# A hybrid SSD, DeltaNet and attention backbone: two-head attention units and chain loads two tiles ahead

## The chip, the cores and the metric

One core of a Trainium2 chip runs the whole program. The metric is the device time of one execution in microseconds; lower is better.

## What is computed

The reference is a backbone of two layers. Each layer normalises and modulates 256 context tokens and 2048 latent tokens, projects them from 1024 to 3100 columns, runs three groups of heads side by side, joins them, projects back and adds the result to the stream. The groups are a state-space scan in both directions (SSD, 6 heads), a gated DeltaNet scan in both directions (4 heads), and softmax attention (6 query heads on 2 key heads, over context and latents). Everything is float32. The attention part, which most of the change is about:

```python
s = jnp.einsum('bqhgd,bkhd->bhgqk', qi, k).astype(jnp.float32) * scale
pr = jax.nn.softmax(s, axis=-1).astype(v.dtype)
return jnp.einsum('bhgqk,bkhd->bqhgd', pr, v)
```

and the DeltaNet recurrence over chunks of 64 tokens, which is serial:

```python
v_new = u_i - jnp.einsum('bhcd,bhde->bhce', w_i, S)
o = jnp.einsum('bhcd,bhde->bhce', qd, S) + jnp.einsum('bhij,bhje->bhie', a_i, v_new)
S = S * d_i[..., None, None] + jnp.einsum('bhcd,bhce->bhde', kd, v_new)
```

## The kernel before, in words

Tokens are cut into 18 tiles of 128 (2 of context, 16 of latents). A layer first runs the input projection (L401, L455), then gating, `gdn_pre` and `gdn_solve` (DeltaNet's triangular systems, on VectorE at L987 and L989 and on GpSimd at L993 and L995), `ssd_states` and `ssd_out` (SSD), `gdn_chain` (the recurrence, tile by tile, both directions at once), and last the output projection (L1231) with the next layer's modulation. Attention is written as generators and runs between all of these.

The order of the instructions on each engine isn't written out. The tile framework schedules them before the program runs, by a timeline of its own, and the order is then fixed; each engine takes its instructions in that order and waits on semaphores. The first eight attention units of a layer stand ahead of `gdn_chain` in the program (L1189) and the rest behind it (L1193).

A unit of attention is one head and 512 queries: 24 such units per layer, and in layer 0 also 6 small ones of 256 context queries. `unit_max` (L516) loads the queries (`q2`, their high parts over their low parts), copies the high half to `qm` on GpSimd (L522), multiplies them with the keys in 20 pieces (`pq`, L531) and takes each piece's maximum over keys on VectorE (`mx`, L533). Small reductions and a sign change give the negated maximum of each query (`nm`, L535, L536); four small fp32 products with the identity turn it into a row (`pm`, L541), which VectorE copies into row 64 of `qm` (L542). `unit_main` (L545) then makes the scores of each of 18 key tiles in two fp32r products (`pst`, L562 and L563; the second brings in the low parts and the negated maximum), takes the exponential on ScalarE (`pe`, L565) and sums the values with these weights (`po`, L556). `v1` holds 65 columns per key head: 64 of the value and one of ones, so that the row sums come out of the same product.

The sum over values comes in two forms. Units 0 to 12 multiply `pe` in plain fp32, one product per tile, which the trace shows as two instructions. From unit 13 on, `pe` and `v1` are split into a high and a low fp32r part (`ph` on ScalarE, L570, `pl` on VectorE, L571; `vh` at L653), and three fp32r products take the place of the fp32 one:

```python
ops = [(v1, pe)] if ph is None else [(vh[0], ph), (vh[1], ph), (vh[0], pl)]
```

In `gdn_chain`, `prep(u)` loads a tile's data through the SP queue (`acv` and others, L1048 to L1055) into pools of two buffers, scales it on VectorE and GpSimd (L1056 to L1061), and makes two sets of 32x32 products on TensorE (`pv`, L1067 and L1076). `step(u)` runs the two halves of a tile; a half takes three turns from TensorE to another engine and back (L1100 to `r` on VectorE; L1114 to `V` on ScalarE; L1123 to `Sc` on VectorE). The loop calls `prep(u + 1)` ahead of `step(u)`:

```python
cur, nxt = nxt, prep(u + 1) if u + 1 < NT else None
S, ox = step(u, S, *cur)
```

`ssd_states` has a product with 64 columns of weights: L789 writes two 64-column halves of one PSUM tile, one after the other, each with 128 rows of weights and 192 moving columns. In `ssd_out`, L816, L839, L840, L845 and L857 are VectorE's part of each tile, and L813, L832, L849, L850, L822 and L858 GpSimd's.

## Time and profile before

| | us |
|---|---|
| median of 3 runs (lowest, highest) | 4039.15 (4035.92, 4040.36) |
| the profiled execution's own time | 4035.59 |
| its span, first to last instruction | 4033.8 |
| TensorE busy (share) | 3776.4 (94%) |
| VectorE busy (share) | 2720.7 (67%) |
| ScalarE busy (share) | 1800.4 (45%) |
| GpSimd busy (share) | 1351.1 (33%) |
| mean granted TensorE clock, share of 2.4 GHz | 0.969 |

PE is TensorE, PEld its loading of weights, DVE VectorE, ACT ScalarE, POOL GpSimd, SP the queue that issues most transfers. Matmuls are pipelined: a row's duration runs from issue to the end and overlaps with the next one's, so what one of them occupies is read from the starts of the rows that follow. The granted clock is a share of 2.4 GHz; its other level is 1.2 GHz, so a mean between 0.5 and 1 is a mix of stretches at either.

### The profile page before, as it was taken

What the parts mean: (1) busy time and instruction counts of PE and PEld (TensorE: products, weight loads), DVE (VectorE), ACT (ScalarE), POOL (GpSimd) and SP (SyncE); (2) the same over time, 40 slices, a digit from 0 to 9 for tenths busy, and PEclk for the clock granted to TensorE, in tenths of its full rate; (3) what the DMA queues carried; (4) which work ended last, traced back from release to release, by engine and by line L of the source; (5) the groups of instructions that cost most, each with busy time, mean ns of one, the idle gap of its engine ahead of it and who ended that gap; (6) DMA issues with size and microseconds to landing.
All of it is one profiled execution on the core that took longest, in us unless ns stands there. A gap on an engine that the chain in (4) does not pass through costs nothing. (4 is left out here: it accounts for less than half of the span.)

```text
span 4033.8 us, 70483 instructions
## 1 busy us (share of the span) xinstructions
PE 3776.4 (94%) x25750; PEld 2839.4 (70%) x25750; DVE 2720.7 (67%) x5372; ACT 1800.4 (45%) x3728; POOL 1351.1 (33%) x1760
## 2 busy tenths in 40 slices
PE   7999999999999888897999999999898999888989
PEld 5899999554566556565678999996554665556667
DVE  6556573789977567774547574746888776667733
ACT  5343332443466455564214443423333655556610
POOL 5112130477476221321213030303774662123100
PEclk9999999999999889998999999999999999989999
DMA  6343432345222544535744433332452215444344
GB/s 202 98 144 112 133 105 95 104 151 173 69 60 60 111 105 103 116 73 181 241 153 130 152 111 130 118 100 77 144 175 72 61 55 118 101 104 120 85 140 154
DMA packets 549798, 477.72 MB, mean 118 GB/s; under 512 B 133128, under 2 KB 487372, under 8 KB 549452
## 3 DMA queue, kind: packets, MB, share of 16 engines
q1 hardware_dynamic: 507596, 437.82, 37.1%
q10 hardware_dynamic: 41856, 35.40, 2.9%
q8 instruction: 203, 3.33, 0.3%
q14 instruction: 143, 1.17, 0.1%
HBM read 328.91 MB, written 144.18 MB: 117 GB/s over the span
## 5 line engine op out<-in xcount | busy, mean ns | idle before, releaser
L565 ACT ACTIVATE pe<-pst 128x512 f32<-128x512 f32 (+1 forms) x876 | 511.8, 594 | 692.0 <-PE pst L563 654.3
L533 DVE TENSOR_REDUCE mx<-pq 128x1 f32<-128x512 f32 (+1 forms) x972 | 590.6, 626 | 131.1 <-PE pq L531 127.0
L531 PE MATMUL pq<-khh,q 128*128 128x512 f32 (+1 forms) x972 | 459.9, 498 | 38.7 <-DVE mx L533 32.1
L556 PE MATMUL po<-pe,v 128*65 128x512 f32 x960 | 488.5, 597 | 0.8 <-ACT os__11676 L579 0.8
L562 PE MATMUL pst<-q,khh 128*128 128x512 f32 (+1 forms) x876 | 429.3, 490 | 16.8 <-DVE mx L533 14.0
L455 PE MATMUL ps<-lo,wh 128*128 128x384 f32 (+2 forms) x1296 | 441.3, 340 | 0.0
L455 PE MATMUL ps<-hi,wl 128*128 128x384 f32 (+2 forms) x1296 | 441.0, 340 | 0.0
L455 PE MATMUL ps<-hi,wh 128*128 128x384 f32 (+2 forms) x1296 | 440.9, 340 | 0.0
L571 DVE TENSOR_TENSOR pl<-pe,ph 128x512 fp32r<-128x512 f32 x396 | 309.6, 786 | 118.6 <-ACT ph L570 54.3
L563 PE MATMUL pst<-qm,klo 65*128 65x512 f32 (+1 forms) x876 | 356.9, 408 | 0.0
L401 PE MATMUL ps<-wh,hi 128*128 128x320 f32 (+1 forms) x1120 | 354.4, 318 | 0.1
L401 PE MATMUL ps<-wl,hi 128*128 128x320 f32 (+1 forms) x1120 | 350.8, 314 | 0.0
L401 PE MATMUL ps<-wh,lo 128*128 128x320 f32 (+1 forms) x1120 | 350.2, 315 | 0.5 <-DVE lo L366 0.5
L531 PEld LDWEIGHTS pq<-khh,q 128*128 128x128 f32 x972 | 186.7, 195 | 190.2 <-DVE mx L533 73.6
L570 ACT CAST ph<-pe 128x512 fp32r<-128x512 f32 x396 | 243.8, 620 | 94.0 <-PE po L556 36.4
L376 DVE TENSOR_TENSOR wl<-wt,wh 128x1024 fp32r<-128x1024 f32 (+3 forms) x144 | 175.3, 1246 | 160.2 <-ACT wh L375 159.8
L556 PE MATMUL po<-ph,vh 128*65 128x512 f32 x792 | 262.2, 413 | 7.7 <-ACT os__20088 L579 4.6
L562 PEld LDWEIGHTS pst<-q,khh 128*128 128x128 f32 x876 | 171.3, 196 | 128.7 <-issue 53.5
L455 PEld LDWEIGHTS ps<-lo,wh 128*128 128x128 f32 x1296 | 244.0, 188 | 10.8 <-issue 0.4
L455 PEld LDWEIGHTS ps<-hi,wh 128*128 128x128 f32 x1296 | 243.5, 188 | 10.3
L455 PEld LDWEIGHTS ps<-hi,wl 128*128 128x128 f32 x1296 | 243.4, 188 | 10.3
L1231 PE MATMUL psd<-woh,mh 128*128 128x512 f32 x544 | 218.7, 402 | 19.0 <-ACT mh L1222 17.6
(588 smaller groups left out, 8136.4 us busy)
## 6 DMA issues: line engine op xcount, KB each, us to landing
wt<-in_w_in_dram SPq DMA_DIRECT2D x72, 512.0 KB
wmt<-in_w_mod_dram SPq DMA_DIRECT2D x48, 512.0 KB
pre_d<-pre SPq DMA_DIRECT2D x34, 512.0 KB
acv<-pre_d SPq DMA_DIRECT2D x34, 512.0 KB
kqc<-kt_d SPq DMA_DIRECT2D x68, 256.0 KB
acv<-pre_d SPq DMA_DIRECT2D x68, 256.0 KB
wt<-in_w_in_dram SPq DMA_DIRECT2D x24, 668.0 KB
wt<-in_w_in_dram SPq DMA_DIRECT2D x24, 640.0 KB
```

The source lines that it names most:

```text
L376: nc.vector.tensor_tensor(out=wl[:, ks, :], in0=wt, in1=wh[:, ks, :].bitcast(F32), op=ALU.subtract)
L401: nc.tensor.matmul(ps, hh[:, k, a], ww[:, k, :], start=(n == 0), stop=(n == 3 * KD - 1))
L455: nc.tensor.matmul(ps, ww[:, k, m * P:(m + 1) * P], hh[:, k, s0:s0 + sn], start=(n == 0), stop=(n == 3 * KD - 1))
L531: nc.tensor.matmul(pq[:, :n], q2[:, u * P:(u + 1) * P], khh[:, kvh, k0t * P + a:k0t * P + a + n], start=True, stop=True)
L533: nc.vector.tensor_reduce(mx[:, i:i + 1], pq[:, :n], axis=AX.X, op=ALU.max)
L556: nc.tensor.matmul(po[0:65, :qn], v[:, kt, vs], p[:, :qn], start=(kt == k0t and j == 0), stop=(kt == k1t - 1 and j == len(ops) - 1))
L562: nc.tensor.matmul(pt[:, :qn], khh[:, kvh, ks], q2[:, :qn], start=True, stop=False)
L563: nc.tensor.matmul(pt[:, :qn], klo[:, kvh, ks], qm[:, :qn], start=False, stop=True)
L565: nc.scalar.activation(out=pe[:, :qn], in_=pt[:, :qn], func=AF.Exp, scale=0.125)
L570: nc.scalar.copy(out=ph, in_=pe)
L571: nc.vector.tensor_tensor(out=pl, in0=pe, in1=ph.bitcast(F32), op=ALU.subtract)
L1231: nc.tensor.matmul(ps, a, w[k][:, n * 512:n * 512 + 512], start=(k == 0 and i == 0), stop=(k == KD - 1 and i == 2))
```

## The change

Units 0 to 7 stay single, now always in plain fp32. The other 16 become eight pairs of two neighbouring heads (`pair_max`, `pair_main`). A pair makes the scores of both heads for a key tile, with two exponentials into one tile `pe` of 128x2x512. Its value products are plain fp32 with 64 columns each, one head into partitions 0 to 63 of `po` and the other into 64 to 127. They are issued in visits of two key tiles, four products in a row, tied behind the last score product. The row sums no longer come out of these products: VectorE adds each new `pe` to `acc` (17 additions of 128x1024 per pair), and at the end two products with ones sum `acc` over its partitions. The splits into `ph`, `pl` and `vh` are gone.

In `unit_max`, `qm`'s high half comes by a second transfer instead of a copy on GpSimd; one reduction per unit takes the place of four and the sign change, and writes into column 64 of a tile that is otherwise zero; the four products that turn it are fp32r with 65 columns of weights; ScalarE copies the row instead of VectorE.

In `gdn_chain`, the transfers of a tile move out of `prep` into `load`, which is called two tiles ahead, and their pools get three buffers.

```diff
-                qm = ap_.tile([65, 512], F32R, name="qm", bufs=3)
-                nc.gpsimd.tensor_copy(qm[0:64, :qn], q2[0:64, :qn].bitcast(F32))
+                    nc.sync.dma_start(qm[0:64, :qn].bitcast(F32), qt_d[0:64, h, q0:q0 + qn])
...
-                    nc.vector.tensor_reduce(nm[:, u:u + 1], mx[:, 0:len(pieces)], axis=AX.X, op=ALU.max)
-                nc.vector.tensor_scalar(out=nm[:, :qn // P], in0=nm[:, :qn // P], scalar1=-1.0, scalar2=None, op0=ALU.mult)
+                nz = nmz[next(turn) % 2]
+                nc.vector.tensor_reduce(nz[:, 0:nu, 64:65], mx[:, 0:nu, 0:len(pieces)], axis=AX.X, op=ALU.max, negate=True)
...
-                    nc.tensor.matmul(pm[64:65, u * P:(u + 1) * P], nm[:, u:u + 1], ident, start=True, stop=True)
-                nc.vector.tensor_copy(qm[64:65, :qn], pm[64:65, :qn])
+                    nc.tensor.matmul(pm[0:65, u * P:(u + 1) * P], nz[:, u, :], identr, start=True, stop=True)
+                nc.scalar.copy(out=qm[64:65, :qn], in_=pm[64:65, :qn])
...
+            def pair_main(h0, q0, qn, k0t, k1t, st):
...
+                def visit(n, behind_mm):
+                    with tc.high_priority():
+                        for v in range(n):
+                            kt, pe = pend.pop(0)
+                            for j in range(2):
+                                c0 = kvh[j] * 65
+                                mm = nc.tensor.matmul(po[half[j]], v1[:, kt, c0:c0 + 64], pe[:, j], start=(kt == k0t), stop=(kt == k1t - 1))
+                                if v == 0 and j == 0:
+                                    behind(mm, behind_mm)
...
+                    pe = ap_.tile([P, 2, 512], F32, name="pe", bufs=PB)
+                    for j in range(2):
+                        pt = aslot("pst")
+                        nc.tensor.matmul(pt, khh[:, kvh[j], ks], st["q2"][j], start=True, stop=False)
+                        mm = nc.tensor.matmul(pt, klo[:, kvh[j], ks], st["qm"][j], start=False, stop=True)
+                        nc.scalar.activation(out=pe[:, j], in_=pt, func=AF.Exp, scale=0.125)
...
+                        nc.vector.tensor_tensor(out=acc, in0=acc, in1=pe, op=ALU.add)
+                    pend.append((kt, pe))
+                    if len(pend) == 3:
+                        visit(2, mm)
...
+                for j in range(2):
+                    nc.tensor.matmul(pl[half[j]], cc("ones")[:, 0:64], acc[:, j], start=True, stop=True)
...
+                units = [(1, un) for un in big[:NS]] + [(2, un) for un in big[NS::2]]
...
+                        xt = gw.tile([P, 2, 4, 32], F32, name="xt_", bufs=3)
+                        kq = gw.tile([P, 2, 4, P], F32, name="kqc", bufs=3)
+                        er = gw.tile([P, 4, P], F32, name="er", bufs=3)
+                        acv = gw.tile([P, 2, 4, 4, 64], F32, name="acv", bufs=3)
...
-                    nxt = prep(0)
+                    ahead = [load(0), load(1)]
+                    nxt = prep(*ahead.pop(0))
                     for u in range(NT):
-                        cur, nxt = nxt, prep(u + 1) if u + 1 < NT else None
+                        if u + 2 < NT:
+                            ahead.append(load(u + 2))
+                        cur, nxt = nxt, prep(*ahead.pop(0)) if ahead else None
```

How the scheduled order moves, at three places. The first is TensorE in the chain of layer 0. Before, the split products of a unit (`po<-ph`, `po<-pl`) stand between the chain's products (`p<-Sc`) and those of a tile's preparation (`pv<-xt`):

```order
L562 MATMUL pst<-q_17963,khh 128x512
L563 MATMUL pst<-qm,klo 128x512
L556 MATMUL po<-ph,vh_17036 65x512
L556 MATMUL po<-ph,vh_17037 65x512
L1067 MATMUL pv<-xt__14053,acv 32x32
L1100 MATMUL p<-Sc,kqc 64x64 x8
L1109 MATMUL p<-Sc,kqc 64x64 x2
L556 MATMUL po<-pl,vh_17036 65x512
L556 MATMUL po<-ph,vh_17036 65x512
L556 MATMUL po<-ph,vh_17037 65x512
L556 MATMUL po<-pl,vh_17036 65x512
```

and now:

```order
L1127 MATMUL pv<-xt__14553,acv 32x32 x16
L613 MATMUL pst<-q_17550,khh 128x512
L614 MATMUL pst<-qm,klo 128x512
L613 MATMUL pst<-q_17704,khh 128x512
L614 MATMUL pst<-qm,klo 128x512
L604 MATMUL po<-pe,v_352 64x512 x4
L613 MATMUL pst<-q_17550,khh 128x512
```

Three products per key tile and head have become one (L604, four in a row for two tiles and two heads). The preparation's first product, of which before one stood alone with other work behind it and the other 15 followed later, now stands with all its 16 together.

The second place is VectorE during SSD in layer 0, one tile's stretch. L840, L839, L845, L857 and L816 belong to SSD, L533 and L535 to attention. Before:

```order
L533 TENSOR_REDUCE mx<-pq 128x1 x2
L857 TENSOR_TENSOR t_9703<-py,t_9703 128x384
L816 SCALAR_TENSOR_TENSOR m_9881<-cst,sp,m_9881 128x128 x6
L533 TENSOR_REDUCE mx<-pq 128x1
L839 TENSOR_TENSOR m_9788<-m_9788,pd 128x384
L845 TENSOR_TENSOR t_9796<-po_9820,ecum 128x192
L845 TENSOR_TENSOR t_9797<-po_9820,ecum 128x192
L861 TENSOR_SCALAR sq<-sq 128x1
L840 TENSOR_TENSOR m_9788<-m_9788,ee 128x384
L533 TENSOR_REDUCE mx<-pq 128x1 x2
```

and now (L896, L895, L901, L913 and L872 are the same lines of SSD; L538 is the maximum and L624 the addition):

```order
L624 TENSOR_TENSOR acc<-acc,pe 128x1024
L538 TENSOR_REDUCE mx<-pq 128x1 x2
L913 TENSOR_TENSOR t_9611<-py,t_9611 128x384
L538 TENSOR_REDUCE mx<-pq 128x1
L872 SCALAR_TENSOR_TENSOR m_9789<-cst,sp,m_9789 128x128 x6
L901 TENSOR_TENSOR t_9704<-po_9728,ecum 128x192
L901 TENSOR_TENSOR t_9705<-po_9728,ecum 128x192
L538 TENSOR_REDUCE mx<-pq 128x1
L895 TENSOR_TENSOR m_9696<-m_9696,pd 128x384
L624 TENSOR_TENSOR acc<-acc,pe 128x1024
```

Between the instructions of one SSD tile stand now additions of 128x1024 beside the maxima. Before, units of this stretch left VectorE nothing but maxima and small reductions.

The third place is the SP queue in the chain of layer 0; the numbers tell the buffers' tiles apart. Before, the transfers of one tile of the chain:

```order
L1054 DMA kqc_13187<-kt_d_94 64x8x128
L1050 DMA xf1_12776<-xd_d_92 32x8x32 x4
L1054 DMA kqc_13187<-kt_d_94 64x8x128
L1034 DMA acv_13189<-pre_d_90 64x2x1024
L1034 DMA acv_13189<-pre_d_90 64x1024 x2
L581 DMA sm_d_99<-os__17337 1x512
L582 DMA mx_d_101<-os__17337 64x512
L1055 DMA er_13551<-eg_d_96 64x4x128 x2
L1052 DMA xt__13549<-xd_d_92 32x8x32 x2
```

and now (L1110 is `kqc`, L1106 `xf`, L1090 `acv`, L1108 `xt_`, L1111 `er`; L526 and L527 are a unit's `q2` and `qm`):

```order
L1110 DMA kqc_13183<-kt_d_94 64x8x128
L1106 DMA xf1_12753<-xd_d_92 32x8x32 x4
L1110 DMA kqc_13183<-kt_d_94 64x8x128
L1090 DMA acv_13185<-pre_d_90 64x2x1024
L1090 DMA acv_13185<-pre_d_90 64x1024 x2
L1108 DMA xt__13545<-xd_d_92 32x8x32 x2
L1111 DMA er_13715<-eg_d_96 64x4x128 x2
L1090 DMA zzg_15087<-zn_d_87 64x2x256
L526 DMA q2_17550<-qt_d_89 128x512
L526 DMA q2_17704<-qt_d_89 128x512
L527 DMA qm_17551<-qt_d_89 64x512
L527 DMA qm_17705<-qt_d_89 64x512
```

The two `xf` buffers have become three (the rows further on write `xf2` and then `xf0`). Each tile is asked for one tile earlier against its use, and a pair's four transfers of queries stand among them instead of a single unit's one.

## Rows read from the trace of the kernel before

**Rows 1.** Page, part 1: busy us, share of the span, instructions, whole span.

```profile
PE 3776.4 (94%) x25750; PEld 2839.4 (70%) x25750; DVE 2720.7 (67%) x5372; ACT 1800.4 (45%) x3728; POOL 1351.1 (33%) x1760
```

**Rows 2.** Busy us (instructions) by stretch: PE, PEld, DVE, ACT, POOL; PEclk, DMA share, GB/s.

```profile
708.00:1031.00 323.00, 299.36 (x1520) 167.35 (x1519) 281.81 (x651) 130.41 (x282) 214.60 (x328) 0.98 0.45 138
1031.00:1346.00 315.00, 302.89 (x1334) 184.11 (x1334) 244.83 (x512) 178.05 (x471) 181.12 (x199) 0.99 0.25 67
1346.00:1792.00 446.00, 393.06 (x5079) 268.13 (x5078) 310.66 (x560) 253.90 (x492) 110.93 (x101) 0.91 0.46 105
1792.00:1860.00 68.00, 61.10 (x251) 41.52 (x250) 40.87 (x63) 46.30 (x77) 3.97 (x3) 0.95 0.29 86
2745.00:3057.00 312.00, 287.14 (x1428) 159.48 (x1428) 267.17 (x610) 124.87 (x265) 205.93 (x317) 0.98 0.43 134
3057.00:3353.00 296.00, 286.77 (x1279) 172.62 (x1275) 231.31 (x477) 162.10 (x430) 161.17 (x182) 0.99 0.23 66
3353.00:3780.00 427.00, 380.62 (x4926) 259.02 (x4927) 304.90 (x549) 252.71 (x488) 109.52 (x97) 0.94 0.44 105
```

**Rows 3.** Busy us of L562 alone by stretch: PE, PEld; PEclk, DMA share, GB/s.

```profile
708.00:1346.00 638.00, 132.92 (x250) 47.55 (x249) 0.98 0.35 103
1346.00:1792.00 446.00, 73.54 (x165) 33.83 (x165) 0.91 0.46 105
```

**Rows 4.** Waits of PE, 1346 to 1792 us: total us, times, longest us.

```profile
PE pv L1067 <- DMA acv<-pre_d: 22.6, 9, 4.8
...
PE pv L1067 <- issue: 7.3, 2, 3.8
PE pv L1067 <- DMA o_d<-ox: 4.3, 1, 4.3
...
PE pv L1067 <- DMA xt__12849<-xd_d: 1.8, 1, 1.8
```

**Rows 5.** VectorE by line, 708 to 1346 us: busy us, mean ns | idle before us.

```profile
L533 DVE TENSOR_REDUCE mx<-pq 128x1 f32<-128x512 f32 (+1 forms) x277 | 166.4, 617 | 46.4 <-PE pq L531 45.9
```

**Rows 6.** Line L840 alone, whole span: duration ns min/median/max.

```profile
L840 DVE TENSOR_TENSOR m<-m,ee x68: 540/756/1384, 1082.8 to 3324.1; 128x384 f32<-128x384 f32 x68
```

**Rows 7.** Timeline of PE, 985 to 1003 us: start us, us, instruction, tile, shape, count.

```profile
986.26 1.02 PE L556 MATMUL po<-pe,v 128*65 128x512 f32 x2
...
987.35 0.40 PE L562 MATMUL pst<-q,khh 128*128 128x512 f32 x1
...
988.39 0.87 PE L789 MATMUL pst<-xd,bn 128*64 128x192 f32 x8
989.19 0.66 PE L776 MATMUL pt<-cst,xb 128*128 128x128 f32 x4
...
995.36 0.55 PE L789 MATMUL pst<-xd,bn 128*64 128x192 f32 x4
995.83 0.66 PE L776 MATMUL pt<-cst,xb 128*128 128x128 f32 x4
```

**Rows 8.** Timeline of PE, 1500 to 1520 us: start us, us, instruction, tile, shape, count.

```profile
1517.86 0.39 PE L556 MATMUL po<-pl,vh 128*65 128x512 f32 x1
...
1518.78 0.63 PE L556 MATMUL po<-ph,vh 128*65 128x512 f32 x2
```

**Rows 9.** Lines by form, whole span: busy us, mean ns | idle before us.

```profile
L571 DVE TENSOR_TENSOR pl<-pe,ph 128x512 fp32r<-128x512 f32 x396 | 309.6, 786 | 118.6 <-ACT ph L570 54.3 <-PE po L556 50.1 <-ACT pe L565 4.0
...
L376 DVE TENSOR_TENSOR wl<-wt,wh 128x1024 fp32r<-128x1024 f32 x72 | 88.3, 1251 | 73.2 <-ACT wh L375 73.2
...
L217 DVE TENSOR_TENSOR wml<-wmt,wmh 128x1024 fp32r<-128x1024 f32 x24 | 46.5, 1939 | 22.8 <-ACT wmh L214 21.7 <-DMA rc<-sr_d 0.9
...
L542 DVE CAST qm<-pm 1x512 fp32r<-1x512 f32 x48 | 33.1, 689 | 42.9 <-PE pm L541 42.2
```

**Rows 10.** Waits of PE, 3353 to 3780 us, the largest: total us, times, longest us.

```profile
PE pv L1067 <- DMA acv<-pre_d: 23.7, 10, 5.0
```

More of the change, by code (lines that the diff above doesn't have):

```diff
@@ L35 @@
 GT = 768
+PB = 6
+NS = 8
 def rev(t):
@@ L525, in unit_max @@
                 pieces = [(a, min(512, kn - a)) for a in range(0, kn, 512)]
-                nm = ap_.tile([P, 4], F32, name="nm")
-                for u in range(qn // P):
-                    mx = ap_.tile([P, 8], F32, name="mx", bufs=4)
+                nu = qn // P
+                mx = ap_.tile([P, 4, 5], F32, name="mx", bufs=2)
+                for u in range(nu):
                     for i, (a, n) in enumerate(pieces):
@@ L648, in attention @@
                         pass
[L649 to L655 removed]
+                at = 0
+                for i, (n, un) in enumerate(units):
                     nxt = ms[i:i + 1] + mb[i + 1:i + 2]
[L657 removed]
+                    left = (24 * units[i + 1][0] if i + 1 < len(units) else 0) + 6 * (i < len(small))
+                    steps = n * (NT - 4)
                     done = 0
[L659 to L660 removed]
+                    for j, _ in enumerate((unit_main if n == 1 else pair_main)(*un, sb[i])):
+                        want = left * (j + 1) // steps
                         adv(nxt, want - done)
@@ L666, in attention @@
                             pass
-                    if i >= 14:
-                        next(side_work, None)
-                    if i % HQ == HQ - 1:
-                        if small and i == HQ - 1:
+                    at += n
+                    for k in range(at - n, at):
+                        if k >= 14:
+                            next(side_work, None)
+                    if at % HQ == 0:
+                        if small and at == HQ:
                             inv(0, LC)
-                        inv(big[i][1], 512)
+                        inv(un[1], 512)
                     yield
@@ L1015, in gdn_chain @@
                     gw = gx.enter_context(tc.tile_pool(reuse_waits="tile", name="gw2", bufs=2))
-                    xf = [gr.tile([P, 2, 4, 64], F32, name=f"xf{i}") for i in range(2)]
-                    for i in range(2):
+                    xf = [gr.tile([P, 2, 4, 64], F32, name=f"xf{i}") for i in range(3)]
+                    for i in range(3):
                         nc.gpsimd.memset(xf[i], 0.0)
```

96 lines of the change are left out of this document (57 added, 39 removed).

## Prediction

> **What bounds the kernel now.** I first read the busy shares of the whole span: TensorE 94%, VectorE 67% [rows 1]. Neither says what a microsecond in attention is worth, because attention shares its stretch with other work. So I cut each layer at its borders, in layer 0 the end of the input projection (708 us), the end of the DeltaNet solve (1031), the first and the last product of the DeltaNet chain (1346, 1792) and the end of attention (1860) [rows 2]. The reader should see that VectorE is busy 281.8 of 323 us up to the solve's end (87%), 244.8 of 315 in the SSD stretch (78%) and 310.7 of 446 in the chain (70%). TensorE shows 393.1 of 446 in the chain at a granted clock of 0.91: part of that stretch ran at 1.2 GHz instead of 2.4.
>
> Next, where attention stands: 250 score products start ahead of the chain, 165 in it [rows 3]; the layer has 444. Last, TensorE's own waits in the chain: 22.6 us for the loads of `acv`, 7.3 for an issue, 4.3 and 1.8 behind two other transfers of the same step [rows 4]. They all end at the product on L1067, the first that reads a freshly loaded tile of the chain. Before the chain VectorE, with the maxima (166.4 us, [rows 5]) and its part of DeltaNet and SSD, is the fuller engine; in the chain it is TensorE with those waits.
>
> **The change, part by part, for one layer.** *Weighted sums.* A plain fp32 product of 512 columns occupies 0.86 us: from 986.26 to 987.35 stand one of them (two instructions) and one fp32r product of 0.23 [rows 7, 8]. A split tile needs three of 0.23, which is 0.69 us [rows 8]. For two 64-wide products beside each other the nearest row is SSD's L789, also fp32, 128 rows by 64 columns of weights, with different moving tiles: two products of 192 columns take 0.47 us (995.36 to 995.83), four take 0.80 (988.39 to 989.19) [rows 7]. A further pair costs 0.33 us, what a single one costs by the 512-column row (192/512 x 0.86 = 0.32), and 0.14 us goes once into entering and leaving. So a visit (two key tiles, two heads) is 2 x 0.86 + 0.14 = 1.86 us, 0.47 per tile and head. Before: 13 plain units x 18 x 0.86 = 201 us and 11 split ones x 18 x 0.69 = 137. After: 8 x 18 x 0.86 = 124 and 8 pairs x 9 visits x 1.86 = 134. That is 80 us less. The ends: without overlap a visit is 3.44 and the gain turns into 34 us of loss; without the 0.14 the gain is 90.
>
> *Row sums and the bias of the maxima.* The two products with ones cost 0.86 + 0.14 per pair, 8 us more. The four small products that turn the bias (512 columns together) go from 0.86 to 0.23, 15 us less. TensorE in all: 87 us less.
>
> *VectorE.* Gone are 198 subtractions of 0.79 us [rows 9], 156 us, and about 1.2 us per unit (three of four small reductions, the sign, the copy of `qm` at 0.69 [rows 9]), 29 us. New are 136 additions of 128x1024 with two SBUF inputs. The nearest rows are the weight splits, also two-input and 128x1024: 1.25 us at L376 in the projection, and 1.94 at L217, where GpSimd does half of the same work at the same time [rows 9]. In SSD, where GpSimd is busy 181.1 of 315 us in 199 instructions [rows 2], the two-input product at L840 has a median of 756 ns against 540 at its shortest [rows 6], so it is stretched there. I take 1.5 us in that stretch and 1.35 in the chain, where GpSimd is busy a quarter of the time; the ends are 1.25 and 1.94. The total hardly moves: about 190 us come, 185 go. The Trainium skill, page "SBUF — State Buffer", section "Who interferes with whom", says that a VectorE instruction with two SBUF inputs and a GpSimd instruction that reads SBUF exclude each other for their whole length. L840's spread agrees. By that rule an addition in SSD meets a GpSimd instruction (mean 0.91 us) in 57% of cases and waits half of it, 1.51 us in all, so the sum would stay; if each waited for a whole one, 2.2 us, it would become rival 2.
>
> *What decides is where they stand.* In the built order of layer 0, 279 score products stand ahead of the chain's first product (before: 250), and 57 additions (before: 3 subtractions). VectorE there: 29 tiles x 20/18 maxima x 0.6 = 19 us, 57 x 1.5 = 86, less 3 x 0.8 and 15 units x 1.2: 84 more. Its 526.6 us become 611. I let it be as full as it is in its fullest stretch, 87%: 702 us instead of 638, **64 longer**. Layer 1: 24 tiles and 54 additions more, 498.5 become 577, 664 instead of 608, **56 longer**. TensorE has no more work there than before (the cheaper pairs pay for the extra tiles), so it follows.
>
> *Chain, layer 0.* 164 split tiles (113 us) become 155 at 0.47 (73): 40 less; nine score pairs 4 less, bias 5 less, row sums 4 more: 45. The waits at L1067: the loads are now issued a step earlier into a third buffer; a step lasts 446/18 = 25 us and the longest wait is 4.8, so all 36 us go [rows 4]. The clock: a mean of 0.91 between its two levels means 18% of the stretch at 1.2 GHz, a loss of 40 us; I take 10 back, a quarter, as the waits are part of the idle time that the low level went with. Together **91 less**, 355 us. VectorE loses 165 x 0.81 and gains 74 x 1.35 there, comes to about 260 us, 73% of the new length, and does not bind. What is late next is its queue: the chain's `r` and `Sc` now stand behind additions of 1.35 us where subtractions of 0.8 stood. Layer 1: 165 tiles become 146, 45 less for the sums, 9 for the scores, 1 for the rest, 24 for the waits (the 23.7 of the one row [rows 10]), 6 for the clock (0.94 there, [rows 2]): **85 less**.
>
> *At no cost:* loading `qm` (54 more DMAs, most of 128 KB) is hidden a unit ahead, as it is asked for together with `q`; were it late, the next unit's scores would be. GpSimd loses as many copies. The SP queue passes nothing new that waits long: the load of a tile waits for the step that has just ended. The tail (68 us, [rows 2]) I leave at 0, within 15 either way: fewer tiles stand in it, but the output products that were mixed with the last tiles now stand behind them.
>
> Sum: 64 + 56 - 91 - 85 = **-56 us** from the profiled execution's 4035.6. That lies 3.6 under the median of the runs shown, so the forecast for a median is 3983.
>
> **Rivals.**
> *1. VectorE is no bound.* It fills to 95% with additions of 1.25: 597/0.95 = 628, 10 us less per layer before the chain, and the chain gives 110 as more of the clock comes back: 4035 - 240 = 3795. For it: 45.9 us of VectorE's idle time before the chain are spent on products for the maxima [rows 5], which TensorE could give sooner. Against: no stretch is fuller than 87%. Chance 0.17.
>
> *2. The other side: the additions collide with GpSimd.* At 1.94 us they are 25 us more before the chain: 636/0.87 = 731, 93 longer, in layer 1 84. The chain then gives about 60 each, as `r` and `Sc` stand behind longer additions: 177 - 120, so 4092. It decides from 1.87 us per addition with the forecast's gain in the chain, from about 1.45 with 60 each. For it: L217, and L840's longest of 1.38 us [rows 6, 9]. Against: GpSimd is busy 57% of SSD and 25% of the chain [rows 2]. Chance 0.20. The Trainium skill's page "SBUF — State Buffer", section "Who interferes with whom", has this as its rule.
>
> *3. No overlap at 512 columns.* A visit of 3.44 gives TensorE 72 x 1.58 = 114 us per layer, uncovered in the chain and about half covered before it: near 4160. L789 speaks against it [rows 7]. Chance 0.04.
>
> *4. The loads are late all the same*, because their issue waits for the step just ended and each step's loads stay as large. 60 us of waits and 16 of clock stay: 4035 + 20 = 4055; half of it: 4017. For it: the waits are on several transfers, not one [rows 4]. Chance 0.09.
>
> **How the numbers follow.** The forecast has 0.50 and its own range is 3910 to 4035. With the rivals the range is 3845 to 4100: below it lies most of rival 1, above it rival 3 and the worst of rival 2. Faster by over 0.2% (8 us, about what a measurement of this kernel can tell from no change): 0.46 of the forecast, rival 1's 0.17 and 0.02 of rival 4, 0.65. Within it: 0.03, 0.02 and 0.04 of the forecast, rival 2 and rival 4, 0.09. Slower: the rest, 0.26.
>
> **What would show it.** Each visit at 1.8 to 2.0 us; additions of 1.35 to 1.6, longer in SSD than in the chain; the counterpart of L1067 no longer waiting for `acv`; the first chain product some 60 us later after the projection's end than now; the chain some 355 us long with a clock of 0.93 or more. The prediction is wrong if the stretch before the chain gets no longer (then VectorE was not its bound), or if the chain stays over 400 us (then its round trips through VectorE and ScalarE set the pace, not TensorE's work).

## The result and the profile after

The change made the kernel **slower**: 4133.85 us (median of 4 runs, 4130.58 to 4144.69) against 4037.94 for the kernel before on the same chip, a ratio of 1.0242 [1.0222, 1.0262]. The forecast was 3983 in a range of 3845 to 4100, so it failed in sign, and the time lies outside the range. The profiled execution took 4144.69 us (span 4142.9), 109 more than that of before.

The busy shares of the page say little again:

```profile
PE 3802.8 (92%) x25214; PEld 2748.3 (66%) x25214; DVE 2713.7 (66%) x4988; ACT 1600.9 (39%) x3384; POOL 1372.4 (33%) x1712
```

Against [rows 1] TensorE has 536 instructions fewer and yet more busy time. The stretches tell why (columns as in [rows 2]; borders: projection end, solve end, first SSD output product, first and last chain product; layer 0, then layer 1):

```profile
701.00:987.00 286.00, 252.40 (x1196) 145.90 (x1195) 242.71 (x541) 109.52 (x237) 189.05 (x298) 0.92 0.41 125
987.00:1135.00 148.00, 138.61 (x589) 71.14 (x587) 119.40 (x219) 61.46 (x131) 30.79 (x32) 0.95 0.29 90
1135.00:1461.00 326.00, 296.17 (x1185) 171.90 (x1185) 258.14 (x452) 161.39 (x430) 178.65 (x179) 0.84 0.22 56
1461.00:1874.00 413.00, 354.62 (x4834) 207.59 (x4834) 244.01 (x376) 159.20 (x327) 109.11 (x93) 0.87 0.51 113
2798.00:3091.00 293.00, 260.97 (x1187) 145.50 (x1186) 241.22 (x535) 107.98 (x228) 187.91 (x296) 0.93 0.38 120
3091.00:3229.00 138.00, 128.69 (x569) 65.12 (x568) 115.08 (x211) 57.58 (x123) 29.81 (x30) 0.96 0.26 81
3229.00:3515.00 286.00, 262.00 (x1069) 158.64 (x1067) 229.63 (x398) 142.17 (x382) 163.32 (x161) 0.81 0.22 58
3515.00:3905.00 390.00, 340.97 (x4646) 198.47 (x4644) 237.09 (x370) 150.96 (x311) 105.74 (x89) 0.87 0.51 115
```

The stretch ahead of the chain takes 760 us instead of 638 and 717 instead of 608; the chain 413 instead of 446 and 390 instead of 427. The rest of the program is some 50 us shorter. The granted clock, 0.98 to 0.99 ahead of the chain before [rows 2], is 0.84 and 0.81 in the SSD stretch; in the chain it fell from 0.91 and 0.94 to 0.87. Time at the low level (1.2 GHz) is 254 us in the whole trace of before and 614 now, summed over the trace's clock records.

**The prices of the single operations were right.** A visit, in TensorE's timeline (start, us), lasts from 1156.39 to 1158.25, 1.86 us as forecast (median of those at full clock: 1.87):

```profile
1156.39 1.94 PE L604 MATMUL po<-pe,v 128*64 128x512 f32 x8
1158.25 0.50 PE L613 MATMUL pst<-q,khh 128*128 128x512 f32 x1
```

The additions, in VectorE's groups by form (busy us, mean ns, idle before), first from 1135 to 1461, then in the chain, take 1.40 and 1.31 us; forecast 1.5 and 1.35:

```profile
L624 DVE TENSOR_TENSOR acc<-acc,pe 128x1024 f32<-128x1024 f32 x45 | 63.2, 1404 | 2.7 <-ACT pe L615 2.7
```

```profile
L624 DVE TENSOR_TENSOR acc<-acc,pe 128x1024 f32<-128x1024 f32 x71 | 92.7, 1305 | 32.2 <-ACT pe L615 31.8
```

**The waits for the loads changed engine.** TensorE's and VectorE's waits in the chain, 1461 to 1874 us (us, times, longest):

```profile
PE pq L536 <- DVE mx L538: 26.7, 9, 4.2
PE p L1160 <- DVE Sc L1187: 14.3, 4, 5.1
PE pst L613 <- DVE mx L538: 8.5, 3, 4.4
PE p L1174 <- DVE r L1164: 4.6, 2, 2.6
PE pv L1127 <- DMA xt__12785<-xd_d: 3.3, 2, 2.4
```

```profile
DVE acv L1121 <- DMA acv<-pre_d: 49.7, 16, 5.0
...
DVE kqc L1116 <- DMA kqc<-kt_d: 16.0, 9, 5.2
```

The counterpart of L1067, now L1127, no longer waits for `acv` [rows 4]. But TensorE stands still just as long, 58 us (413 less 355 busy, against 53 before), behind `mx`, `Sc` and `r` of VectorE; and VectorE waits 50 us for `acv` at L1121, the mask. Before, VectorE waited for loads as well, mostly at the scaling of `kqc`, 42 us in these two rows of 1346 to 1792 us against 66 now:

```profile
DVE kqc L1056 <- DMA kqc<-kt_d: 35.4, 13, 3.7
...
DVE acv L1061 <- DMA acv<-pre_d: 6.3, 4, 2.2
```

One place in the change where it stops TensorE, VectorE's timeline, then TensorE's:

```profile
1576.65 0.42 DVE L1164 TENSOR_TENSOR r<-acv,p 128x256 f32<-128x256 f32 x1
1582.12 0.69 DVE L1121 TENSOR_TENSOR acv<-acv,msk 128x512 f32<-128x512 f32 x1 [5.05 <-DMA acv<-pre_d]
1582.73 1.28 DVE L538 TENSOR_REDUCE mx<-pq 128x1 f32<-128x512 f32 x2
```

```profile
1579.50 0.40 PE L614 MATMUL pst<-qm,klo 65*128 65x512 f32 x1
1583.46 1.18 PE L536 MATMUL pq<-khh,q 128*128 128x512 f32 x2 [3.56 <-DVE mx L538]
```

The mask waits 5.05 us for its load, the maxima stand behind it, their banks stay taken, and TensorE stops for 3.56. It is the mask of tile 7 (counted from 0), with ten `Sc` done, which is five steps: two tiles ahead of its use. Before, the mask of tile 7 (1511.2 us) stood behind twelve. The scheduler had handed the slack of the third buffer on to the load's first reader.

### The profile page after: what moved, and what is told of

Its sections match the earlier page's. It is cut to its first block, busy times and chain, and to the rows that moved or that the text cites. A ratio compares the mean times of both kernels' runs of the same rounds, so it can differ in the third digit from the quotient of the medians.

```text
span 4142.9 us, 68151 instructions
## 1 busy us (share of the span) xinstructions
PE 3802.8 (92%) x25214; PEld 2748.3 (66%) x25214; DVE 2713.7 (66%) x4988; ACT 1600.9 (39%) x3384; POOL 1372.4 (33%) x1712
## 5 line engine op out<-in xcount | busy, mean ns | idle before, releaser
L538 DVE TENSOR_REDUCE mx<-pq 128x1 f32<-128x512 f32 (+1 forms) x972 | 582.5, 625 | 151.2 <-PE pq L536 148.6
L615 ACT ACTIVATE pe<-pst 128x512 f32<-128x512 f32 x576 | 333.9, 596 | 475.8 <-PE pst L614 471.4
L536 PEld LDWEIGHTS pq<-khh,q 128*128 128x128 f32 x972 | 195.9, 210 | 323.9 <-DVE mx L538 160.1
L624 DVE TENSOR_TENSOR acc<-acc,pe 128x1024 f32<-128x1024 f32 x256 | 339.6, 1326 | 70.0 <-ACT pe L615 68.4
L604 PE MATMUL po<-pe,v 128*64 128x512 f32 x1152 | 353.5, 708 | 0.0
L613 PE MATMUL pst<-q,khh 128*128 128x512 f32 x576 | 285.0, 495 | 33.7 <-DVE mx L538 24.6
L558 PE MATMUL po<-pe,v 128*65 128x512 f32 x600 | 308.3, 606 | 1.3 <-ACT os__12287 L574 0.6
L566 ACT ACTIVATE pe<-pst 128x512 f32<-128x512 f32 x300 | 172.6, 589 | 295.2 <-PE pst L564 293.6
L614 PE MATMUL pst<-qm,klo 65*128 65x512 f32 x576 | 250.6, 435 | 0.0
L1294 PE MATMUL psd<-woh,ml 128*128 128x512 f32 x544 | 217.6, 401 | 1.5 <-DVE ml L1287 0.8
```

The lines of the kernel that those rows point to most:

```text
L536: nc.tensor.matmul(pq[:, :n], q2[:, u * P:(u + 1) * P], khh[:, kvh, k0t * P + a:k0t * P + a + n], start=True, stop=True)
L538: nc.vector.tensor_reduce(mx[:, u, i:i + 1], pq[:, :n], axis=AX.X, op=ALU.max)
L558: nc.tensor.matmul(po[0:65, :qn], v1[:, kt, kvh * 64:kvh * 64 + 65], pe[:, :qn], start=(kt == k0t), stop=(kt == k1t - 1))
L604: mm = nc.tensor.matmul(po[half[j]], v1[:, kt, c0:c0 + 64], pe[:, j], start=(kt == k0t), stop=(kt == k1t - 1))
L613: nc.tensor.matmul(pt, khh[:, kvh[j], ks], st["q2"][j], start=True, stop=False)
L614: mm = nc.tensor.matmul(pt, klo[:, kvh[j], ks], st["qm"][j], start=False, stop=True)
```

## The experiments

Stretches of every profiled run in us: "ahead" from the projection's end to the chain's first product, "chain" from there to its last `Sc`, layer 0 / layer 1. Ratios are to the kernel before on the same chip. Its own medians on these chips lie between 4030 and 4038 us, so a difference between two runs' medians can be off by as much as 8 us.

| run | ahead | chain | median us | ratio, 95% interval |
|---|---|---|---|---|
| before | 638 / 608 | 446 / 428 | 4037.94 | |
| after | 760 / 717 | 413 / 390 | 4133.85 | 1.0242 [1.0222, 1.0262] |
| e1 | 750 / 726 | 333 / 326 | 4007.8 | 0.9943 [0.9922, 0.9964] |
| e2 | 732 / 683 | 407 / 373 | 4055.84 | 1.0052 [1.0036, 1.0068] |
| e3 | 758 / 723 | 489 / 456 | 4200.23 | 1.0417 [1.0383, 1.0451] |
| e4 | 645 / 605 | 387 / 370 | 3997.93 | 0.9909 [0.989, 0.9929] |
| e5 | 762 / 756 | 348 / 339 | 4028.92 | 0.9993 [0.997, 1.0017] |
| e6 | 689 / 658 | 310 / 309 | 3857.52 | 0.9569 [0.954, 0.9598] |
| e7 | 642 / 603 | 334 / 330 | 3901.98 | 0.9681 [0.9651, 0.9711] |
| e8 | 687 / 660 | 429 / 423 | 4035.72 | 1.0009 [0.9992, 1.0026] |
| e9 | 761 / 721 | 338 / 323 | 3996.65 | 0.991 [0.9881, 0.9939] |
| e10 | 734 / 688 | 305 / 312 | 3907.32 | 0.9686 [0.9664, 0.9708] |
| e11 | 691 / 662 | 400 / 385 | 4020.73 | 0.9967 [0.9951, 0.9983] |
| e12 | 730 / 670 | 341 / 329 | 3936.67 | 0.9762 [0.9741, 0.9783] |
| e13 | 755 / 720 | 376 / 361 | 4168.74 | 1.0335 [1.0317, 1.0353] |
| e14 | 689 / 646 | 322 / 320 | 3852.88 | 0.9551 [0.9534, 0.9568] |
| e15 | 629 / 597 | 343 / 342 | 3922.29 | 0.9724 [0.9706, 0.9743] |
| e16 | 686 / 655 | 338 / 331 | 3895.26 | 0.9654 [0.9633, 0.9675] |
| e17 | 761 / 710 | 338 / 324 | 4001.34 | 0.9915 [0.99, 0.993] |
| e18 | 688 / 661 | 311 / 303 | 3856.02 | 0.9556 [0.954, 0.9572] |

### The chain's loads and who reads them first

**e1, the first readers held one tile ahead.**

```diff
-nc.vector.tensor_tensor(out=kq[:, 0], in0=kq[:, 0], in1=er, op=ALU.mult)
+mm = nc.vector.tensor_tensor(out=kq[:, 0], in0=kq[:, 0], in1=er, op=ALU.mult)
+if last_S:
+    behind(mm, last_S[-1])
...
+last_S.append(nc.vector.tensor_tensor(out=Sn, in0=sd, in1=pc, op=ALU.add))
```

The mask is held in the same way; GpSimd's scaling of `kqc` stands behind the last `sd`.

> The changed kernel, with the first readers of a tile's loads on VectorE and GpSimd (the mask on acv, the two scalings of kqc) held in order behind the end of the step before the last, so that they stand one tile ahead of their use as they did before the change, while the loads stay two tiles ahead. Theory A (the load waits went from TensorE to VectorE's queue, where the maxima stand behind them, so TensorE pauses and its clock falls): VectorE's waits for acv and kqc in the chain fall from 66 us to under 15, the chains become 40 us shorter each (412 to about 370, 390 to about 350), the clock in the chain rises above 0.90, and the time is 4040 to 4075. Theory B (the additions fill VectorE) and theory C (the side-by-side products themselves lower the clock): the waits go, but something else ends next, 4115 to 4145.

The chains fell to 333 and 326 us, further than theory A had it, and the time by 126 us (121 by the two ratios). Theory C (the products side by side lower the clock) is out: the same pairs now run in the chain at 0.96 and 1.00. The windows of both chains, and what is left of VectorE's waits for loads from 1451 to 1784 us:

```profile
1451.00:1784.00 333.00, 322.50 (x4833) 192.20 (x4833) 252.09 (x376) 158.19 (x326) 118.06 (x93) 0.96 0.66 140
...
3438.00:3764.00 326.00, 312.48 (x4690) 182.84 (x4685) 249.97 (x366) 154.86 (x319) 105.34 (x89) 1.00 0.60 137
```

```profile
DVE acv L1123 <- DMA acv<-pre_d: 3.3, 1, 3.3
```

Layer 0 can be read straight off the windows: 413 less 354.6 busy is 58 us of pauses, 333 less 322.5 is 10; that is 48. Busy time fell from 354.6 to 322.5 with the same 155 key tiles in the stretch, as the clock rose from 0.87 to 0.96; that is 32. Together the 80 us. Here the pauses cost once themselves and once the clock. The time ahead of the chain hardly moved: what happens there has another cause.

**e3 and e4, the loads' own share.** e3 is the change with the old loads (two buffers, `prep(*load(u + 1))`); e4 the kernel before with the new ones.

> The changed kernel with the chain's loads as they were before (one tile ahead, two buffers), all the rest as changed. If the loads two tiles ahead brought what the prediction put to them (60 us of waits, 16 us of clock), this is 70 us slower, about 4205. Theory A: the waits only change their place, from VectorE's queue back to TensorE's, and the time stays within 30 us of 4134.

> The kernel before, with nothing but the chain's loads two tiles ahead in three buffers. The prediction's step: TensorE's waits for acv (36 and 24 us) go and some clock comes back, about 3965. Theory A: the masks move two tiles ahead in VectorE's queue as well and wait there, TensorE pauses on products behind VectorE instead, and the time is within 25 us of 4038.

Theory A failed here in its size: without the early loads the change is 66 us slower (the waits for `acv` are back on TensorE), close to the other expectation's 4205, and on their own they bring 0.9%. So the early loads are worth something even when VectorE waits for them; e4's chains gain 59 and 58 us. e3 shows one thing more: with the old loads the changed kernel's chains are 489 and 456 us, 43 and 28 longer than before. In layer 0 TensorE's pauses are 77 us there instead of 53, and the clock is 0.80 instead of 0.91. The waits that the early loads had to take away had grown with the rest of the change. Both kernels show the wait where A puts it (e3's TensorE, e4's VectorE from 1353 to 1740 us):

```profile
PE pv L1127 <- DMA acv<-pre_d: 38.2, 13, 7.1
```

```profile
DVE kqc L1060 <- DMA kqc<-kt_d: 41.6, 14, 4.5
DVE acv L1065 <- DMA acv<-pre_d: 18.2, 10, 3.9
```

**e7, e4 with the first readers held** (the edit of e1).

> The kernel of e4 (the kernel before with the loads two tiles ahead) with the first readers on VectorE and GpSimd held one tile ahead, as in e1. Theory A: VectorE's waits for the loads go here too, the chains fall from 387 and 370 us to about 350 and 340, the time is 3920 to 3960. Rival (with subtractions of 0.8 us instead of additions in VectorE's queue there is slack enough, so the wait costs nothing): within 10 us of e4's 3998.

3902, beyond theory A's range: the chains fell another 53 and 40 us, with the clock at 0.98 and 1.00. The wait costs the split units as well, though less than the pairs (80 and 64 us from the changed kernel to e1); it needs no additions in the queue. In the kernel before the scalings of `kqc` had waited as well, unnoticed, since TensorE's waits were read alone.

```profile
1348.00:1682.00 334.00, 324.18 (x4906) 222.10 (x4907) 275.75 (x495) 223.45 (x439) 113.79 (x100) 0.98 0.62 138
```

### What lengthens the stretch ahead of the chain

**e2 and e10, no additions** (in the change and in e1): the sums of the paired units are taken from a tile of ones.

```diff
-                    elif kt == k0t + 1:
-                        acc = ap_.tile([P, 2, 512], F32, name="acc", bufs=1)
-                        nc.vector.tensor_tensor(out=acc, in0=pend[0][1], in1=pe, op=ALU.add)
-                    else:
-                        nc.vector.tensor_tensor(out=acc, in0=acc, in1=pe, op=ALU.add)
+                    else:
+                        acc = one
```

> The changed kernel without its 136 additions per layer: the row sums of the pairs are taken from a constant tile of ones, so the softmax of the 16 paired units is left without its true sums. Theory B: VectorE loses some 180 us per layer, the stretch ahead of the chain falls from 760 and 717 us to about 650 and 620, the clock in the SSD stretch comes back to 0.95 or more, and the time is under 3950. Theory C: the clock stays at 0.80 to 0.88 wherever pairs run, and the time falls by 60 us at most, to 4070 or above. Theory A: the chains stay at about 400 and 380 us, because VectorE still waits for acv there; only the stretch ahead of the chain can gain.

> The kernel of e1 without its additions, as in e2 (the row sums of the paired units come from a constant tile of ones). Read with e1 it gives the additions' own price once the load waits are out of the way. Theory E: VectorE's volume isn't what limits, so the stretch ahead of the chain stays within 30 us of e1's 750 and 726 and the clock in SSD under 0.92; the time is 3930 to 3990. Rival (additions block the queue): 3850 or less, with the stretch ahead of the chain near 690.

Theory B falls: e2 gets 29 and 34 us back ahead of the chain, not 100, and layer 0's SSD stretch keeps a clock of 0.84; its chains stay at 407 and 373, as theory A had it. With the load waits gone (e10) the additions cost 100 us in all, 54 of them ahead of the chains, and the time came out between the two expectations. Its SSD stretch, from 1123 us, has VectorE busy 64% of the time and TensorE still busy 270 of 286 us, at a clock of 0.84:

```profile
1123.00:1409.00 286.00, 269.83 (x1082) 160.38 (x1083) 183.93 (x384) 148.73 (x408) 156.54 (x175) 0.84 0.18 52
```

**e6, pairs only in the chain:** e1 with

```diff
-NS = 8
+NS = 14
```

> The kernel of e1 with 14 single units and 5 pairs instead of 8 and 8, so that only single units stand in the SSD stretch and all pairs in the chain. If the pairs are what lengthens the stretch ahead of the chain (750 and 726 us in e1, 638 and 608 before), it comes back to 640 to 670 and 610 to 640, with a clock of 0.95 or more; the chain, with more tiles at 0.86 us each, is 350 to 390: 3900 to 3960. Rival (the new maxima and the order that comes with them lengthen it): it stays above 700 and the time is 3990 to 4050.

The time and the chains are below the expectation; the stretch ahead is above it, and level with e8's (687 and 660), which has no pairs at all. The SSD stretch is what it was before, 236 us at a clock of 0.99, and the stretch ahead 61 and 68 us shorter than e1's. First e6, then e1, over the 18 SSD output tiles:

```profile
1126.00:1362.00 236.00, 227.62 (x1003) 144.11 (x1002) 182.93 (x382) 142.04 (x392) 158.22 (x168) 0.99 0.20 58
```

```profile
1129.00:1423.00 294.00, 265.35 (x1074) 155.25 (x1074) 236.65 (x421) 150.58 (x408) 171.90 (x168) 0.85 0.17 50
```

At full clock both hold the same TensorE work: 227.6 x 0.99 = 225 us, 265.4 x 0.85 = 226. The 58 us between them are 20 more of pauses (28.7 against 8.4) and nearly all the rest clock. Pauses of over half a microsecond: 19 with pairs, 4 with single units.

**e5, e17, e9, e13: what it is about the pairs.** All four start from e1. e5 visits after every key tile, e17 takes the visits' priority away, e9 swaps the loops over key tiles and heads, and e13 does every product twice, so that the weighted sums of the paired units are doubled:

```diff
 e5
-                    if len(pend) == 3:
-                        visit(2, mm)
+                    if len(pend) == 2:
+                        visit(1, mm)
 e17
-                    with tc.high_priority():
 e9
-                        for v in range(n):
-                            kt, pe = pend.pop(0)
-                            for j in range(2):
+                        take = [pend.pop(0) for v in range(n)]
+                        for j in range(2):
+                            for v, (kt, pe) in enumerate(take):
 e13
+                                for w in range(2):
```

> The kernel of e1 with a visit after every key tile instead of after every second one (four instructions instead of eight). Theory D: the clock falls in SSD and stays low because the visits come in lumps of 1.87 us with stretches of SSD's own small products between them, in which one pause is enough to lose the clock and busy time alone does not bring it back. Then the clock of the SSD stretch rises from 0.85 to 0.93 or more, the stretch ahead of the chain loses 30 us or more per layer, which outweighs 20 us for entering and leaving twice as often: 3950 to 3990. Rival (the clock only follows VectorE's waits, however the visits are cut): the clock stays near 0.85 and the time is 4015 to 4040.

> The kernel of e1 with the visits no longer at high priority in the scheduler's eyes (they keep their place behind the scores of a tile). Theory G: at high priority each lump of 1.87 us is put ahead of SSD's own products, whose next step waits, so SSD's round trips through VectorE, ScalarE and GpSimd get longer and TensorE pauses in them; single units are mere filler there. Then the SSD stretch's clock comes back to 0.93 or more, the stretch ahead of the chain is 690 to 720 and 655 to 690 us instead of 750 and 726, and the time is 3930 to 3970. Rival (the place is fixed by the scores anyway, and the pair's own round trip through exponentials and banks makes the pauses): 735 to 755 and 710 to 730, and the time is 3990 to 4020.

> The kernel of e1 with the products of a visit in another order: both key tiles of one head, then both of the other, so that neighbours write the same partitions and can overlap only once instead of four times; a visit costs TensorE about 3.0 instead of 1.87 us, 20 visits in the SSD stretch about 22 us more. Theory E (in the SSD stretch the pairs leave TensorE too little work to cover VectorE's bursts, and what the overlap saves is lost again as pauses and a lower clock): the stretch ahead of the chain changes by less than 12 us, with a clock in the SSD stretch of 0.90 or more instead of 0.85; the chain, where TensorE is the fuller engine, is about 40 us longer. Rival F (TensorE's work sets the SSD stretch): the stretch ahead of the chain grows by 25 us or more and its clock stays.

> The kernel of e1 with every product of a visit done twice into the same sums (the weighted sums of the 16 paired units come out doubled). A visit then takes TensorE about 3.6 us at full clock instead of 1.87, whatever overlaps with what; that is some 35 us more work in each SSD stretch and some 60 us more in each chain. Theory E (in the SSD stretch the pairs leave TensorE too little work to cover the bursts of the other engines; what they save is lost as pauses and a lower clock): the stretch ahead of the chain grows by less than 15 us in each layer, with the clock of the SSD stretch at 0.92 or more instead of 0.85. Rival F (TensorE's work sets the SSD stretch at whatever clock): it grows by 30 us or more and the clock stays near 0.85. The chain gets 40 to 60 us longer in both: 4090 to 4190.

Theory D is out: at twice the visits the clock stayed (0.86 and 0.78) and the time rose 21 us. Theory G is out: 761 and 710 us, the clock at 0.84 and 0.83. e9 didn't do what it was for: with the key tiles of one head next to each other a visit still takes 1.87 us (the last section has the reason). e13 did: a visit takes 3.63 us, and the stretches ahead of the chain stayed at 755 and 720. That is theory E's figure, but not its clock (0.87 and 0.88, not 0.92), and 264 instead of 279 score tiles stand ahead of the chain in layer 0: the scheduler moved part of the load behind. So the pairs' own products don't set that stretch, but "too little work" isn't shown either. **Open** is what in the pair makes VectorE, ScalarE and TensorE wait for each other more often: additions account for 54 of 129 us (e10), neither the size of the visits, nor their priority, nor their TensorE time for the rest. In layer 0's SSD stretch no single wait stands out: in e1 TensorE waits 10.7 us for maxima (5.4 in e6), 9.0 for SSD's own steps on VectorE (1.3) and 6.5 for exponentials (1.2). Scores and maxima take turns in the same few PSUM banks; their number was not varied.

### What the parts are worth

**e8, only the new maxima; e12, e6 with the old ones** (the lines of `unit_max` taken from one kernel into the other).

> The kernel before with nothing but the new maxima of a unit (the bias products as fp32r with the copy on ScalarE, one small reduction, qm by transfer). By the prediction's prices (15 small products of 0.63 us less per layer and 29 us of VectorE less) it gains up to 40 us, 3990 to 4030. Rival (the states move behind the solve and the stretch ahead of the chain gets longer, as in the changed kernel): 4040 to 4100, with the stretch at 660 to 700 us.

> The kernel of e6 with the maxima of a unit as they were before the change (plain fp32 bias products, sign and copy on VectorE, qm copied by GpSimd). In e8 the new maxima lengthened the stretch ahead of the chain by 49 and 52 us and gave it back behind the chain. If that is a mere shift of attention work, this kernel has 640 to 650 and 605 to 620 us ahead of the chain, a longer chain or tail, and the time is within 20 us of e6's 3858. If the shift costs, it is 3800 or less.

Ahead of the chain e8 is 49 and 52 us longer, as its rival said; `ssd_states` now stands behind the solve, and 286 instead of 250 score tiles are done there in layer 0. Of the 49 us 39 are TensorE's own work at full clock, moved ahead; behind that stretch e8 gives the same back. No gain in all. In e12, with the load waits gone, the old maxima cost 79 us, and the stretch ahead is 730 and 670 us instead of shorter: neither expectation. So the new maxima by themselves don't set its length. e12 has the old ones, `ssd_states` behind the solve all the same, and 278 score tiles ahead (e6: 268); e15 below has the new ones, no pairs, most of `ssd_states` ahead of the solve's end as before, 236 tiles and a stretch of 629 and 597 us. How much attention the scheduler puts there goes some of the way, but not all: e8 has more tiles there than e12 and is shorter.

**e11, e6 with the first readers free.**

> 14 single units and 5 pairs as in e6, but the first readers of the loads free, as in the change. If the two causes (masks that wait for loads in VectorE's queue; pairs in the SSD stretch) add up, this is e6 plus what e1 gained in the chains (80 and 64 us): the stretch ahead of the chain as in e6 (689, 658), the chains 370 to 390, the time 3960 to 4000. If the masks only hurt because additions stand behind them, which e6 also has, nothing changes in this forecast; if pairs in SSD were the cause of the long chain as well, the chain is 310 to 330 and the time near 3870.

Layer 0's chain is 400 us and the time 4021, both above the forecast; layer 1's 385 is within it. Freeing the readers costs 163 us here, more than in e1 (126).

**e14, e7 with the new maxima; e15, no pairs (`NS = 24` in e1); e16, `NS = 16`; e18, e6 without priority.**

> The kernel of e7 (before, loads two tiles ahead, first readers held) with the new maxima of e8, so everything of the change but the pairs, and the readers held. If the new maxima are worth something only once the load waits are gone (as between e12 and e6, 79 us), the time is 3820 to 3860 and the pairs bring nothing beyond split units; if they are only worth something together with the pairs, it is 3890 to 3910.

> The kernel of e1 with all 24 units single and plain fp32: no pairs, no additions, no split. TensorE pays 0.86 us per tile and head everywhere (some 60 us more per layer in the chain than with pairs), VectorE loses the additions. If pairs in the chain are worth their price, this is slower than e6's 3858 by 40 us or more, with a chain of 340 to 370; if the additions eat what the products save, it is within 20 us of e6.

> The kernel of e6 with 16 single units and 4 pairs instead of 14 and 5. The stretch ahead of the chain stays (685 to 695 and 655 to 665), and two units at 0.86 instead of 0.47 us per tile cost the chain 14 us of TensorE per layer, while 17 additions go: within 25 us of e6's 3858. If pairs were a loss in the chain too, it is 3840 or less.

> The kernel of e6 (14 single units, 5 pairs, first readers held) with the visits no longer at high priority. In the chain the same lumps stand ahead of the chain's own products: if theory G holds there, the chains of 310 and 309 us lose another 10 us or more each and the time is under 3840; if the order within the chain is set by the chain itself, it stays within 10 us of 3858.

e14 has no pair at all, units 13 to 23 split as before, and runs in 3852.88 us, 4.5% under the kernel before and level with e6 and e18 (3857.52, 3856.02). With the load waits out of the queue the new maxima are worth 49 us there (e7 to e14), and pairs in the chain bring nothing beyond split units. They do beat plain units: with no pair at all (e15) the time is 65 us above e6, as expected, and with one pair fewer (e16) 38, more than expected. e18's chains lost some 2 us on the mean, so the visits' priority isn't what sets the order there. The chain of e14, layer 0:

```profile
1394.00:1717.00 323.00, 316.89 (x4891) 219.50 (x4890) 269.50 (x459) 230.27 (x453) 111.33 (x93) 1.00 0.64 142
```

## Why the prediction was wrong

**"All 36 us go" [rows 4]: the step that failed in the chain.** The forecast took TensorE's waits for `acv` as the loads' whole price and gave the chains 91 and 85 us less; they came out 33 and 37 shorter. Its first term, TensorE's work, was right: counted at full clock (busy time weighted by the granted clock), work in the chain fell from 356 to 310 us in layer 0 and from 357 to 298 in layer 1, 45 and 59 less where 45 and 55 were forecast. The other two had the wrong sign. TensorE's pauses, of which 36 and 24 us were to go, rose from 53 to 58 and from 46 to 49; the loss to the low clock, of which 10 and 6 were to come back, rose from 38 to 45 and from 25 to 44. The forecast asked who waited for the loads before, not who would read them first afterwards. VectorE's mask and scaling went two tiles ahead along with the loads and waited there (66 us in layer 0), with `mx`, `r` and `Sc` in the same queue. The forecast had named that queue as "what is late next", but for the length of the additions, not for a DMA wait. Its own sign of being wrong, a chain over 400 us, came in layer 0. With the readers held (e1) the chains are 113 and 102 us shorter than before: the sums, the scores, the waits and the clock together were not overrated.

**"I let it be as full as it is in its fullest stretch, 87%": the term that was too small ahead of the chain.** 64 and 56 us were forecast, 122 and 109 measured. VectorE's busy time there was forecast nearly right, 611 and 577 us against 620 and 586. (56 more maxima stand ahead of layer 0's chain than before; the forecast counted 32.) What failed was turning that work into time by a share. No addition stands in the solve, from which the 87% came; all 57 of layer 0 stand behind it, where VectorE was 78% full [rows 2]. With 78% the same 84 us of work would have given 84 / 0.78 = 108, but that would have been luck: e10 shows that VectorE's volume isn't the mechanism, since without the additions most of the length remains. By TensorE's account of layer 0, 18 of the 122 us are more work at full clock (592 to 610), 38 more pauses (36 to 73) and 67 the low clock (10 to 77). The pairs in SSD are worth 61 and 68 us of the excess (e1 against e6). The rest, some 50 us per layer, stands in e6 and e8 and not in e15. Part of it is attention that the scheduler placed ahead of the chain (in layer 0 TensorE's own work is 25 us of it in e6 and 39 in e8); why the scheduler does so, and the rest, stays open.

**"TensorE has no more work there than before ... so it follows"** was nearly right about work (18 and 11 us more at full clock) and wrong about time: it took the clock for given. It didn't ask for the clock ahead of the chain at all, and the fall there is the largest single loss.

**The rivals.** Rival 2 had the sign, at 4092, but not the mechanism: additions took 1.40 us, less than the 1.45 and 1.87 from which it would decide. By the Trainium skill's page "SBUF — State Buffer", section "Who interferes with whom", an addition came to 1.51 us as an estimate; the 1.40 measured lie between that and 1.25 undisturbed. Rival 4 ("the loads are late all the same") was nearest in the chain, but saw the wait stay on TensorE. Rival 1 is excluded by the longer stretch, rival 3 by the visits.

**The tail**, set at 0 within 15, gave back some 45 us in the two layers: fewer tiles were left behind the chain (10 in layer 0, 30 before).

## What to carry to other kernels

When loads are moved earlier, look at every engine's first reader of them, not only at the one that waits now: where a scheduler lays out in-order queues, it moves the reader along, and a reader that waits blocks all behind it. Hold it at the place where the data is needed; here one ordering edge per reader was worth 126 us, more than the 96 by which the change was slower. And cost a stretch at the clock that it will have: saved TensorE work that leaves pauses is paid again at 1.2 GHz.

## What the runs showed of the hardware

**A 64-row fp32 product is cheap only beside one of the other half.** In the changed kernel a visit is sometimes split by SSD's products. One product alone (two instructions) holds TensorE for 1.00 us, two of different heads (four instructions, one product into each half of `po`) for 1.01, four for 1.87; all at full clock. The timeline of the change:

```profile
1174.61 1.07 PE L604 MATMUL po<-pe,v 128*64 128x512 f32 x2
1175.61 0.88 PE L912 MATMUL py<-xn,m 128*128 128x64 f32 x6
...
1424.15 1.08 PE L604 MATMUL po<-pe,v 128*64 128x512 f32 x4
1425.16 0.59 PE L898 MATMUL po<-S,bc 64*128 64x192 f32 x2
```

In e13, where neighbours are the same product twice into the same half, two of them alone hold it for 1.86:

```profile
1184.26 1.93 PE L605 MATMUL po<-pe,v 128*64 128x512 f32 x4
1186.12 0.66 PE L913 MATMUL py<-xn,m 128*128 128x64 f32 x4
```

The single product's two instructions start 480 ns apart, and a following one of the same half starts 0.43 us behind the second; two products of different halves start 7 ns apart. So the price by itself is about that of 65 rows, 0.86 us [rows 7], and the pair halves it: the forecast had the right number from L789 and the right reason. e9's order (two key tiles of one head, then two of the other, by the program) doesn't take the overlap away:

```profile
1091.68 1.94 PE L604 MATMUL po<-pe,v 128*64 128x512 f32 x8
1093.56 0.61 PE L536 MATMUL pq<-khh,q 128*128 128x512 f32 x2
```

Its eight instructions start at 0, 13, 481, 493, 910, 923, 1339 and 1352 ns, two rows of starts 13 ns apart. That fits the second head starting beside the first although it stands behind both of its products; the trace doesn't name the halves, so this is read from the times alone.

**TensorE can stay at the low level while it is busy.** In the change the clock fell behind pauses of 0.62, 0.69 and 0.21 us between 1243.9 and 1246.8 us. TensorE then worked at 1.2 GHz from 1247.2 to 1260.9 without a gap, mostly on SSD's products and last on a visit (1256.65 to 1260.27), and the clock rose at 1260.9:

```profile
1247.20:1257.00 9.80, 9.80 (x33) 7.17 (x33) 5.87 (x15) 3.96 (x12) 6.63 (x6) 0.50 0.20 60
1257.00:1260.80 3.80, 3.80 (x10) 1.01 (x7) 2.15 (x5) 0.86 (x3) 0.00 (x0) 0.50 0.00 0
1261.00:1274.60 13.60, 13.15 (x65) 8.48 (x65) 12.04 (x19) 8.63 (x25) 11.09 (x11) 1.00 0.15 43
```

The Trainium skill, page "TensorE: Matmul & The Clock Gate", section "What's actually happening", has activity lift the clock and idle time lower it. The fall at 1247.2 agrees, it stands behind pauses. The busy 13.7 us at the low level show that activity didn't lift it at once here; what ended them was not tried.
